# Conditions' blocks on TensorE in four column places, with later loads in the third layer and later states' products in the first

## The chip, the core and the metric

The kernel runs on one core of a Trainium2 chip. The metric is device time in microseconds (us) of one execution; lower is better. Five engines work at once: TensorE (PE, with its weight loads listed as PEld), VectorE (DVE), ScalarE (ACT), GpSimd (POOL) and SyncE (SP). SP, POOL and ACT also issue the transfers (DMA), and a queue issues in order: an issue that waits holds up those behind it.

## The reference, cut to what matters

One step of a diffusion backbone with four layers: a bidirectional state-space scan (SSD), a gated MLP, a second state-space layer (S5) and neighbourhood attention. It works on 128 context tokens and 512 latent tokens of width 1024. Before each layer the two conditions (one for context tokens, one for latent tokens) give shift, scale and gate:

```
mod = silu(cond) @ w_mod[i] + b_mod[i]          # cond: (2, 1024), w_mod[i]: (1024, 3072)
shift, scale, gate = split(mod, 3)
u = (rms_norm(x) * g * (1 + scale) + shift) @ w_in[i]
x = x + gate * (mixer(u) @ w_out[i])
```

So for each of four layers a 2 x 1024 matrix is multiplied by a 1024 x 3072 matrix in float32. The kernel does it in 24 blocks of 512 output columns, six for each layer; a block has 8 tiles of 128 x 512 weights, 2 MB, which are loaded from memory.

## The kernel before, in words

**Large products.** Each projection is a list of units (8 weight tiles of 128x128, 512 KB). `stream` (L326) plays them on TensorE in slots: one slot is six matmuls, two halves of 320 tokens by three terms of a split into high and low parts. `play` takes the order of TensorE from a table written by hand: `put(slot, work)` lets `work` issue its instructions after that slot. TensorE's order is always that of the table. The order of DVE, ACT and POOL is the table's too in the third layer (`ALSO5`); elsewhere, and for SP everywhere, a planner decides it by its own costs. `unit` turns a loaded weight tile (`raw`, 2 buffers) into high and low parts: ACT writes both, and POOL issues a transfer that adds the raw tile to the low part (`wlo<-raw`).

**The conditions' blocks.** `mod_pe` (L388) makes four blocks of the first layer on TensorE before the first projection: the stationary operand is 128x2 (`self.cs`, two conditions), the moving operand a 128x512 weight tile, 8 of them for a block. The other 20 blocks are made beside other work by `mod_ew` (L406), a generator that `tick` advances: two in the first layer's scan, four in its output projection (`leave(0)`), two at the start of the MLP (L1193 to L1198), and six in each of `leave(1)` and `leave(2)`. There DVE does 16 passes for a block over 128x512 elements (L437, L439) into the accumulator `wacc`; TensorE then turns the two sums in 8 transposes of 128x128 (L417), and DVE reduces them (L418). `mod_b` adds the bias. The loads (`wm`, 512 KB each) are asked for one at a time, two ahead.

**The first layer's scan.** Eight groups of heads follow each other on TensorE, 48 slots apart (L944 to L961). In a group, `begin` loads the state H and the decays, `turn` transposes five chunks and DVE makes the weighted copy `xw` (L1047), `context` and `advance` multiply into states (L1077), `off` multiplies states by C (L1112), and `diag` does the part within a chunk (L1068). `tables` at the start makes the step sizes (L804 to L874).

**The third layer.** For 16 items the input side loads matrices (`load_in`, tile `ix`, 3 buffers), transposes them and drives the states (`drive`); DVE steps through the scan (L1768, L1771). The output side loads (`load_out`), generates (`gen`, tiles `gx`), copies states (`take`), multiplies (`answer`), forms a kernel `KK`, spreads it in 8 small transfers on SP's queue (`unroll`, L1842), and multiplies it by the input `ur` (`within`, L1851). `IN5` and `OUT5` hold the slots of these steps, counted from the item's own.

Of the kernel before, what the change touches and what calls it, by code (L numbers as in the profile page):

```python
# [117 lines left out]
class Net:  # L118
# [235 lines left out]
    def cond(self):  # L354
# [7 lines left out]
        nc.vector.tensor_tensor(self.cs, x, t, op=OP.mult)  # L362

# [6 lines left out]
    def mod_w(self, i, nb, k, n, p, bufs, tag="wm"):  # L370

        w = p.tile([128, n, 512] if tag == "wm" else [128, 2, T], F32, tag=tag, bufs=bufs, name=self.n("wm"))[:, 0:n, 0:512]
        self.nc.sync.dma_start(w, self.I["w_mod"][i, nb, k // 2, :, k % 2:k % 2 + n])
        return w
# [12 lines left out]

    def mod_pe(self, i, p, blocks=range(6), bufs=4, n=1):  # L388

        nc = self.nc  # L390
        for nb in blocks:
            q = self.bank("pmod")
            for k0 in range(0, 8, n):
                w = self.mod_w(i, nb, k0, n, p, bufs)
                for j in range(n):
                    k = k0 + j
                    nc.tensor.matmul(q[:2, :], self.cs[:, k, :], w[:, j, :], start=(k == 0), stop=(k == 7))
            r = p.tile([2, 512], F32, tag="modr", bufs=1, name=self.n("modr"))
            nc.scalar.copy(r, q[:2, :])
            q = self.bank("pmodt")  # L400
            for j in range(4):
                nc.tensor.transpose(q[:, 2 * j:2 * j + 2], r[:, 128 * j:128 * j + 128], self.ident[:2, :2])
            self.mod_b(i, nb, q[:, 0:8].rearrange("p (a b) -> p a b", b=2))
            yield

    def mod_ew(self, i, p, blocks=range(6), bufs=2, tags=("wm", "wacc"), pacc=None):  # L406


        nc = self.nc
        e = nc.vector  # L410

        def total(nb, acc):
            q = self.small([128, 4, 2], "modq")
            for c in range(2):
                t = self.bank("pmod")
                for j in range(4):
                    self.nc.tensor.transpose(t[:, 128 * j:128 * j + 128], acc[:, c, 128 * j:128 * j + 128], self.ident)  # L417
                e.tensor_reduce(q[:, :, c], t.rearrange("p (a b) -> p a b", a=4), axis=AX.X, op=OP.add)  # L418
            self.mod_b(i, nb, q)
        todo = [(nb, kb) for nb in blocks for kb in range(4)]  # L420
        load = lambda s: self.mod_w(i, todo[s][0], 2 * todo[s][1], 2, p, bufs, tags[0])
        ws = [load(s) for s in range(bufs - 1)]
        done = None
        for s, (nb, kb) in enumerate(todo):
            w = ws.pop(0)
            if s + bufs - 1 < len(todo):
                ws.append(load(s + bufs - 1))
            if kb == 0:
                acc = (pacc or p).tile([128, 2, 512] if tags[1] == "wacc" else [128, 2, T], F32, tag="s5gx" if pacc else tags[1],
                                       bufs=2 if pacc else 2 if tags[1] == "wacc" else bufs,  # L430
                                       name=self.n("wacc"))[:, :, 0:512]
            for j in range(2):
                k = 2 * kb + j
                for c in range(2):
                    a = self.cs[:, k, c:c + 1]
                    if k == 0:
                        e.tensor_scalar(acc[:, c], w[:, j], a, 0.0, op0=OP.mult, op1=OP.add)  # L437
                    else:
                        e.scalar_tensor_tensor(acc[:, c], w[:, j], a, acc[:, c], op0=OP.mult, op1=OP.add)  # L439
# [1854 lines left out]
```

## Time and profile before

| | |
|---|---|
| median of 3 runs | 3027.43 us (3025.84 to 3032.1) |
| profiled execution: time | 3024.37 us |
| profiled execution: first to last instruction (span) | 3022.4 us |
| granted TensorE clock, mean | 0.956 |
| TensorE busy | 2747.4 us, 91% |
| VectorE busy | 2085.6 us, 69% |
| ScalarE busy | 1478.1 us, 49% |
| GpSimd busy | 1275.1 us, 42% |

The profiled execution lies 3.1 us under the median. A share over the whole span is a mean over very different stages: the scan of the first layer until about 600 us, its output projection until 733, the MLP until 1183, its output projection until 1311, the third layer until 2091, its output projection until 2237, the attention until 2889, and the last output projection. A stage has its own limit, so a number is read in its stage.

### The profile page before, as it was taken

Reading aid. Unit: us, or ns where it says so; the run is one execution under the profiler, and the core shown is the slowest. Engines: PE = TensorE matmul, PEld = TensorE weight load, DVE = VectorE, ACT = ScalarE, POOL = GpSimd, SP = SyncE. Lnnn points to the kernel's source line nnn. Section 1 sums busy time; section 2 is a strip of 40 time slices with the busy share of each in tenths; the row PEclk is TensorE's granted clock in tenths of the full one; section 3 lists DMA queues with packets and bytes.
Section 4 is the critical chain, followed back from the end, with each engine's and each line's share of the span. In section 5 each row is a group of like instructions: output and inputs, shape, how many; then the busy total and the mean of one; then the engine's idle time right before and its main releaser. Section 6 shows DMA issues by size and latency. Waiting matters only on the chain.

```text
span 3022.4 us, 50482 instructions
## 1 busy us (share of the span) xinstructions
PE 2747.4 (91%) x18412; PEld 2636.6 (87%) x18412; DVE 2085.6 (69%) x4948; ACT 1478.1 (49%) x2525; POOL 1275.1 (42%) x1452
## 2 busy tenths in 40 slices
PE   6879989999988888989898876999899999999998
PEld 3768989899988888989898775999889999999998
DVE  5987776676679887735888972225957777777842
ACT  5534434534443444356675553444136666666641
POOL 4466667512576663123443540223343333333332
PEclk9989999999999999999898887999999999999999
DMA  7666667797676667967676569324525444444342
GB/s 254 170 182 164 174 164 192 191 288 220 172 215 194 164 194 227 278 184 219 164 221 169 147 172 186 106 92 135 202 86 148 133 135 131 136 129 135 111 181 85
DMA packets 271734, 517.91 MB, mean 171 GB/s; under 512 B 77888, under 2 KB 146944, under 8 KB 270464
## 3 DMA queue, kind: packets, MB, share of 16 engines
q1 hardware_dynamic: 240512, 411.93, 44.5%
q0 software_dynamic: 24064, 87.04, 14.9%
q10 hardware_dynamic: 6912, 15.73, 1.4%
q8 instruction: 146, 2.39, 0.3%
q14 instruction: 100, 0.82, 0.1%
HBM read 333.83 MB, written 65.70 MB: 132 GB/s over the span
## 4 chain that ended last, share of the span: by engine, by line
PE 31%; DVE 25%; DMA 13%; POOL 9%; ACT 8%; issue 7%; SPq 1%; ACTq 0%; POOLq 0%; DVEq 0%
PE acc L326 25%; DMA wlo<-raw 4%; DVE S L1771 3%; DVE wacc L439 2%; DVE sl L1768 2%; DVE e L2077 2%; DVE cacc L915 2%; POOL dd L1022 2%; POOL dd L1029 2%; ACT e L2075 1%; DMA raw<-in_w_mlp_dram 1%; DVE sb L2072 1%; DMA raw<-in_w_out_dram 1%; DVE pt L205 1%; DVE yn L2108 1%
## 5 line engine op out<-in xcount | busy, mean ns | idle before, releaser
L326 PE MATMUL acc<-hhi,whi 128*128 128x320 f32 (+2 forms) x3472 | 624.2, 319 | 25.4 <-DVE x L610 10.2
L326 PE MATMUL acc<-hlo,whi 128*128 128x320 f32 (+2 forms) x3472 | 633.0, 319 | 2.5 <-DVE hlo L579 1.3
L326 PE MATMUL acc<-hhi,wlo 128*128 128x320 f32 (+2 forms) x3472 | 613.9, 318 | 6.8 <-DMA wlo<-raw 6.8
L326 PEld LDWEIGHTS acc<-hhi,whi 128*128 128x128 f32 (+1 forms) x3472 | 542.7, 193 | 35.3 <-issue 14.6
L326 PEld LDWEIGHTS acc<-hhi,wlo 128*128 128x128 f32 (+1 forms) x3472 | 544.8, 194 | 13.2 <-DMA wlo<-raw 8.7
L326 PEld LDWEIGHTS acc<-hlo,whi 128*128 128x128 f32 (+1 forms) x3472 | 544.7, 193 | 7.9 <-DVE hlo L579 2.8
L226 POOL DMA_DIRECT2D wlo<-raw x164 | 145.1, 891 | 541.8 <-ACT wlo L225 491.9
L205 POOL TENSOR_TENSOR wlo<-raw,whi 128x1024 fp32r<-128x1024 f32 x95 | 244.6, 2576 | 262.9 <-ACT whi L204 86.7
L227 ACT CAST whi<-raw 128x1024 fp32r<-128x1024 f32 (+1 forms) x164 | 170.6, 1041 | 244.8 <-DMA raw<-in_w_mlp_dram 100.3
L225 ACT ACTIVATE wlo<-raw 128x1024 fp32r<-128x1024 f32 (+1 forms) x164 | 173.2, 1057 | 168.7 <-DMA raw<-in_w_mlp_dram 87.9
L439 DVE SCALAR_TENSOR_TENSOR wacc<-wm,conds,wacc 128x512 f32<-128x512 f32 x280 | 224.7, 855 | 30.4 <-DMA wm<-in_w_mod_dram 30.4
L326 PE MATMUL acc<-y,whi 128*128 128x320 f32 (+2 forms) x1024 | 175.8, 312 | 7.1 <-DVE y L746 3.1
L1771 DVE TENSOR_TENSOR S<-S,sl 128x32 f32<-128x32 f32 x1008 | 176.4, 230 | 0.0
L204 ACT CAST whi<-raw 128x1024 fp32r<-128x1024 f32 x125 | 129.2, 1046 | 76.0 <-PE acc L326 67.8
L326 PEld LDWEIGHTS acc<-y,whi 128*128 128x128 f32 x1024 | 155.5, 188 | 10.6 <-DVE y L746 4.5
L2077 DVE TENSOR_SCALAR e<-e,mx 128x384 f32<-128x384 f32 (+1 forms) x160 | 154.1, 963 | 4.2
L915 DVE SCALAR_TENSOR_TENSOR cacc<-pad,vec,cacc 128x644 f32<-128x644 f32 x128 | 144.2, 1127 | 2.2 <-ACT cacc L913 0.9
L2075 ACT ACTIVATE e<-sb,mx 128x384 f32<-128x384 f32 x128 | 79.0, 617 | 107.3 <-DVE mx L2074 106.6
L1768 DVE TENSOR_TENSOR sl<-S,A 128x64 f32<-128x64 f32 x504 | 120.9, 280 | 0.0
L1889 DVE TENSOR_TENSOR y<-y,sg 128x640 f32<-128x640 f32 x16 | 14.1, 879 | 150.2 <-ACT sg L1888 150.2
L1547 POOL TENSOR_TENSOR s5gy<-Bu,Qt 128x512 f32<-128x512 f32 x64 | 90.0, 1438 | 57.3 <-DVE s5gx L1557 53.9
L1022 POOL TENSOR_TENSOR dd<-cmat,dt 128x512 f32<-128x512 f32 x80 | 108.2, 1358 | 12.2 <-DVE dt L826 9.4
(407 smaller groups left out, 5381.9 us busy)
## 6 DMA issues: line engine op xcount, KB each, us to landing
wlo<-raw POOLq DMA_DIRECT2D x163, 512.0 KB, 5.4
wm<-in_w_mod_dram SPq DMA_DIRECT2D x96, 512.0 KB, 6.5
raw<-in_w_out_dram SPq DMA_DIRECT2D x64, 512.0 KB, 4.5
raw<-in_w_nat_dram SPq DMA_DIRECT2D x64, 512.0 KB, 3.8
raw<-in_w_ssd_dram SPq DMA_DIRECT2D x48, 512.0 KB, 3.5
raw<-in_w_mlp_dram SPq DMA_DIRECT2D x48, 512.0 KB, 3.6
fb<-fd SPq DMA_DIRECT2D x40, 512.0 KB, 5.4
s5X<-s5gx SPq DMA_DIRECT2D x32, 512.0 KB, 4.8
```

The costliest lines, as they stand in the source:

```text
L204: (hi_eng or nc.scalar.copy)(hi, src)
L205: (lo_eng or nc.vector).tensor_tensor(lo, src, f(hi), op=OP.subtract)
L225: self.nc.scalar.activation(lo, raw, AF.Copy, scale=-1.0)
L226: self.nc.gpsimd.dma_start(lo, raw, accum_op=OP.add)
L227: self.nc.scalar.copy(hi, raw)
L326: mm(p[:m, o:o + c], w[:, kt, :], v(hx), start=(k == 0 and wi == 0), stop=(k == 8 * len(units) - 1 and wi == 2))
L439: e.scalar_tensor_tensor(acc[:, c], w[:, j], a, acc[:, c], op0=OP.mult, op1=OP.add)
L915: nc.vector.scalar_tensor_tensor(acc, pad[:, j:j + 644], w(j), acc, op0=OP.mult, op1=OP.add)
L1022: nc.gpsimd.tensor_tensor(dg.rearrange("p (h l) -> p h l", h=4), N.ident[:, None, :].to_broadcast([128, 4, 128]), self.dt[:, c, 32 * d + 4 ...
L1768: e.tensor_tensor(t[d], F[:, d, at[d], None, :].to_broadcast([128, 2, 32]), A[:, :, d], op=OP.mult)
L1771: e.tensor_tensor(dst[d], dst[d], t[d][:, k].rearrange("p (r g) -> p r g", r=2)[:, ::1 - 2 * k], op=OP.add)
L2077: nc.vector.tensor_scalar(e[:, :w], e[:, :w], m[:, 3:4], None, op0=OP.mult)
```

## The change

Every condition block goes to TensorE. `self.csx` is the conditions with zeros behind; a stationary operand is now 32 columns of it, of which two are the conditions of this tile, and the others give sums that nobody reads. Tile k writes to the output partitions 32*(k%4) to 32*(k%4)+31. `mod_end` sums the four places and transposes in one: four products of 128 columns of the copy `r` with `sel`, a 128x2 matrix that is one where the partition modulo 32 is 0 or 1. In `mod_ew` the four loads of a block are asked for together, right after the products of the block before; products are issued at every fourth tick, and `mod_end` one tick after the ACT copy. The tick times stay.

```diff
+    def mod_sums(self, ws):
+        q = self.bank("pmod")
+        for k, w in enumerate(ws):
+            o = 32 * (k % 4)
+            self.nc.tensor.matmul(q[o:o + 32, :], self.csx[:, 2 * k:2 * k + 32], w, start=(k < 4), stop=(k >= 4))
+        return q
+    def mod_end(self, i, nb, r):
+        q = self.bank("pmodt")
+        for j in range(4):
+            self.nc.tensor.matmul(q[:, 2 * j:2 * j + 2], r[:, 128 * j:128 * j + 128], self.sel, start=True, stop=True)
+        self.mod_b(i, nb, q[:, 0:8].rearrange("p (a b) -> p a b", b=2))
...
     def mod_pe(self, i, p, blocks=range(6), bufs=4, n=1):
         for nb in blocks:
+            ws = [self.mod_w(i, nb, k, n, p, bufs) for k in range(0, 8, n)]
+            q = self.mod_sums([w[:, j, :] for w in ws for j in range(n)])
+            r = p.tile([128, 512], F32, tag="modr", bufs=1, name=self.n("modr"))
+            self.nc.scalar.copy(r, q)
+            self.mod_end(i, nb, r)
...
+    def mod_ew(self, i, p, blocks=range(6), tags=("wm", "modr"), more=None):
+        lend = lambda: more[0].tile([128, 2, 512], F32, tag=more[1], bufs=2, name=self.n("wm"))
+        load = lambda nb: [self.mod_w(i, nb, 2 * kb, 2, p, MB if more else 4, tags[0], lend if more and kb == 3 else None)
+                           for kb in range(4)]
+        blocks = list(blocks)
+        ws, done = load(blocks[0]), None
+        for n, nb in enumerate(blocks):
             yield
+            if done:
+                self.mod_end(i, *done)
+                done = None
+            yield
+            yield
+            q = self.mod_sums([w[:, j, :] for w in ws for j in range(2)])
...
+            self.nc.scalar.copy(r, q)
+            done = nb, r
+            if n + 1 < len(blocks):
+                ws = load(blocks[n + 1])
+            yield
+        self.mod_end(i, *done)
         yield
...
-            put(t - 2, self.begin, N, P)
+            put(t + 2, self.begin, N, P)
...
-            put(t + 5, self.context, N, P)
-            for j, s in enumerate((1, 2 * TA + TS, 4 * TA + TS, 4 * TA + 2 * TS + 1)):
+            put(t + 10, self.context, N, P)
+            for j, s in enumerate((1, 2 * TA + TS + 2, 4 * TA + TS + 2, 4 * TA + 2 * TS + 3)):
                 if j:
                     put(t + s - 3, self.fade, N, P, j)
                     put(t + s, self.advance, N, P, j)
-                put(t + s + TS + (4 if j else 0), self.off, N, P, j)
+                put(t + s + TS + 4, self.off, N, P, j)
...
-IN5 = (-3, -1, 1, 4, 9, 12)
-OUT5 = (-15, 0, -5, 0, 5, 7, 9, 17)
+IN5 = (-2, -1, 1, 5, 9, 12)
+OUT5 = (-10, 0, -5, 0, 5, 7, 9, 19)
...
-                put(e + IN5[s], self.load_in, P, s)
+                for d in range(2):
+                    put(e + (2 if s == d == 1 else IN5[s]), self.load_in, P, s, d)
...
                 put_(o + OUT5[0], self.load_out, P)
+                put_(o + 6, self.load_again, P)
...
-                put_(o + OUT5[6] + 3, self.unroll, P)
+                put_(o + OUT5[6] + 2, self.unroll, P)
                 put_(o + OUT5[7], self.within, P)
...
     def load_out(self, N, P):
-        P["ur"] = self.load_u(N, kt)
...
+    def load_again(self, N, P):
+        P["ur"] = self.load_u(N, P["kt"])
```

In the MLP and in `leave(1)` the fourth tile of a block and the copy `r` borrow buffers of other tags (`s5gx`, `wacc`), since `wm` has three there. In `leave(2)` tiles and copies lie in the buffers `ya` and `yb`.

## Rows read from the trace of the kernel before

**Rows 1.** The page: two engines, the costliest condition group, and the condition loads
```profile
PE 2747.4 (91%) x18412; PEld 2636.6 (87%) x18412; DVE 2085.6 (69%) x4948; ACT 1478.1 (49%) x2525; POOL 1275.1 (42%) x1452
...
L439 DVE SCALAR_TENSOR_TENSOR wacc<-wm,conds,wacc 128x512 f32<-128x512 f32 x280 | 224.7, 855 | 30.4 <-DMA wm<-in_w_mod_dram 30.4
...
wm<-in_w_mod_dram SPq DMA_DIRECT2D x96, 512.0 KB, 6.5
```

**Rows 2.** Busy time by stretch: length, busy us (instructions) by engine, then clock, DMA
```profile
core 0: us, PE busy (x) PEld busy (x) DVE busy (x) ACT busy (x) POOL busy (x), PEclk, DMA share, GB/s
62.00:200.00 138.00, 110.31 (x709) 104.16 (x707) 124.27 (x148) 67.80 (x106) 68.89 (x50) 0.90 0.66 175
200.00:585.00 385.00, 353.03 (x2433) 332.33 (x2431) 270.74 (x299) 166.46 (x265) 255.02 (x215) 0.96 0.69 174
626.00:716.00 90.00, 89.30 (x619) 88.78 (x618) 62.34 (x103) 29.99 (x34) 10.41 (x12) 1.00 0.94 275
1202.00:1291.00 89.00, 89.00 (x618) 88.78 (x616) 69.40 (x118) 28.22 (x30) 10.52 (x12) 1.00 0.93 274
2091.00:2207.00 116.00, 106.57 (x711) 106.03 (x710) 113.10 (x139) 24.28 (x29) 49.81 (x15) 0.96 0.55 185
2904.00:2991.00 87.00, 86.74 (x591) 86.47 (x590) 19.40 (x24) 20.38 (x24) 28.91 (x12) 1.00 0.37 128
1320.00:1820.00 500.00, 432.76 (x3041) 424.30 (x3040) 373.41 (x1690) 303.64 (x504) 209.53 (x331) 0.91 0.67 182
```

**Rows 3.** TensorE's groups by form: count, busy us, mean ns, idle before
```profile
L1112 PE MATMUL off<-c,H 128*128 128x128 f32 x256 | 34.4, 279 | 10.4 <-DVE H L1101 10.1 <-DVE y L1071 0.2
L1068 PE MATMUL yd<-dd,xb 128*64 128x128 f32 x320 | 26.3, 285 | 0.7 <-ACT off L1084 0.7
L417 PE MATMUL pmod<-cmat,wacc 128*128 128x128 f32 x160 | 22.1, 281 | 1.0 <-DVE wacc L439 1.0
```

**Rows 4.** TensorE in order of time, setup stage: start, us, instructions
```profile
30.27 1.28 PE L469 MATMUL cols<-ones,ssum 128*128 128x1 f32 x10
...
33.44 7.03 PE L397 MATMUL pmod<-wm,conds 128*2 128x512 f32 x16
```

**Rows 5.** GpSimd in order of time, setup stage (columns as in Rows 4)
```profile
46.86 1.86 POOL L226 DMA_DIRECT2D wlo<-raw x2
```

**Rows 6.** What TensorE waited for from 62 to 200 us: total, times, longest
```profile
PE G L1054 <- DVE xw L1047: 7.9, 2, 7.3
PE stc L1077 <- DVE xw L1047: 7.1, 1, 7.1
PE dtT L823 <- DVE dtv L816: 3.3, 1, 3.3
PE G L1054 <- DVE y L1071: 3.0, 1, 3.0
```

**Rows 7.** The same from 200 to 585 us
```profile
PE st L1077 <- DVE xw L1047: 4.3, 4, 1.3
PE stc L1077 <- DVE xw L1047: 3.7, 2, 2.1
```

**Rows 8.** TensorE in order of time in the third layer's output projection
```profile
2125.59 3.54 PE L326 MATMUL acc<-hhi,whi 128*128 128x320 f32 x12 [6.56 <-DVE x L610]
...
2190.65 3.77 PE L326 MATMUL acc<-hhi,whi 128*128 128x320 f32 x16 [2.87 <-DVE x L610]
```

**Rows 9.** What TensorE waited for most from 1320 to 1820 us
```profile
PE t L1851 <- DMA tr<-KK: 33.5, 9, 7.2
```

**Rows 10.** What SP's queue waited for in the same stretch
```profile
SPq L1794 <- DVE gx L1544: 63.6, 10, 14.8
SPq L1695 <- PE mT L1708: 54.8, 22, 5.2
SPq L1842 <- ACT KK L1836: 37.5, 9, 6.0
```

**Rows 11.** Busy time from the first scan to the last (columns as in Rows 2)
```profile
1390.00:1800.00 410.00, 350.34 (x2456) 343.50 (x2455) 358.51 (x1663) 247.93 (x402) 195.62 (x310) 0.90 0.65 179
```

More of the change, by code (lines that the diff above doesn't have):

```diff
@@ L362, in cond @@
         nc.vector.tensor_tensor(self.cs, x, t, op=OP.mult)
+        self.csx = c.tile([128, 48], F32, name="condsx")
+        nc.vector.memset(self.csx, 0.0)
+        nc.vector.tensor_copy(self.csx[:, 0:16], self.cs.rearrange("p k c -> p (k c)"))
+        self.sel = c.tile([128, 2], F32, name="sel")
+        nc.sync.dma_start(self.sel, self.I["consts"][:, 664:666])
     def mod_tiles(self, i):
@@ L388, in mod_pe @@
     def mod_pe(self, i, p, blocks=range(6), bufs=4, n=1):
-        nc = self.nc
         for nb in blocks:
[L392 to L403, printed above, removed]
-            yield
@@ L406, in mod_ew @@
[L406 to L439, printed above, removed]
-            yield
-            if kb == 1 and done:
-                total(*done)
-            if kb == 3:
-                done = nb, acc
-                if pacc:
-                    total(*done)
-                    done = None
-        if done:
-            total(*done)
@@ new lines, in mod_pe @@
+            ws = [self.mod_w(i, nb, k, n, p, bufs) for k in range(0, 8, n)]
[3 more added lines that the diff above has]
+            self.mod_end(i, nb, r)
+            yield
+    def mod_ew(self, i, p, blocks=range(6), tags=("wm", "modr"), more=None):
[5 more added lines that the diff above has]
+        for n, nb in enumerate(blocks):
+            yield
+            if done:
[4 more added lines that the diff above has]
+            q = self.mod_sums([w[:, j, :] for w in ws for j in range(2)])
+            if more:
+                r = lend()[:, 0]
+            elif tags[1] == "modr":
+                r = p.tile([128, 512], F32, tag="modr", bufs=1, name=self.n("modr"))
+            else:
+                r = p.tile([128, 2, T], F32, tag=tags[1], bufs=4, name=self.n("modr"))[:, 0, 0:512]
+            self.nc.scalar.copy(r, q)
[4 more added lines that the diff above has]
+        self.mod_end(i, *done)
@@ L661, in leave @@
             self.rest = i == 0
-            self.put_beside(self.mod_ew(i + 1, self.tp, blocks, bufs=4 if mod else MB, tags=mod or ("wm", "wacc")))
+            self.put_beside(self.mod_ew(i + 1, self.tp, blocks, tags=mod or ("wm", "modr"), more=(self.tp, "wacc") if i == 1 else None))
             for s in range(4 * len(blocks) + 4):
@@ L1195, in groups @@
             mod = []
-            put(RM[0] - 1, lambda: mod.append(N.mod_ew(1, self.tp, (4, 5), MB, pacc=N.tp)))
+            put(RM[0] - 1, lambda: mod.append(N.mod_ew(1, self.tp, (4, 5), more=(N.tp, "s5gx"))))
             for k in range(10):
@@ L1690, in load_u, with load_in @@
         return ur
-    def load_in(self, N, P, s):
-        for d in range(2):
-            x = P["in", s, d] = self.tile(N, [128, 4, 128], "ix", BI)
-            N.nc.sync.dma_start(x, N.s5X[2 * P["kt"] + s][:, d])
+    def load_in(self, N, P, s, d):
+        x = P["in", s, d] = self.tile(N, [128, 4, 128], "ix", BI)
+        N.nc.sync.dma_start(x, N.s5X[2 * P["kt"] + s][:, d])
     def gen(self, N, P, s):
@@ L2131 @@
     NVEC += _w
-NCONST = 664
+NCONST = 666
 def net(ctx, tc, I, O, layers=(0, 1, 2, 3)):
@@ L2196, in layout @@
                                   i[:, None] <= i, i[:, None] >= i, i[:, None] > i, i[:, None] < i,
-                                  i[:, None] // 8 == i[:16]], 1).astype(np.float32)
+                                  i[:, None] // 8 == i[:16], i[:, None] % 32 == i[:2]], 1).astype(np.float32)
     r["w_mod"] = np.ascontiguousarray(a["w_mod"].reshape(4, 4, 2, 128, 6, 512).transpose(0, 4, 1, 3, 2, 5))
```

10 lines of the change are left out of this document (6 added, 4 removed).

## The prediction, made before the changed kernel ran

> **What bounds the kernel now.** First the busy shares [rows 1]: TensorE is busy 2747 of 3022 us, so at most 275 us are idle, and DVE is busy 2086 us, of which the passes over the condition blocks are 225 us. A share of the span doesn't tell what they are worth, so next comes the busy time by stretch [rows 2]. Read two columns against each other, TensorE and DVE. In the first scan's opening (62 to 200 us) DVE has 124 of 138 us, TensorE 110: DVE sets the pace. In the scan's later part TensorE has 353 of 385. In the middle of the output projections of layers one and two (the 90 and 89 us stretches) TensorE has no idle time at all, and transfers fill 0.94 and 0.93 of the 16 engines. In the third layer's output projection DVE has 113 of 116 us, TensorE 107. The last projection, which has no condition blocks, gives the undisturbed rate: 591 matmuls in 86.74 us, 0.147 us each, or 0.88 us for a slot of six. The third layer has 67 us without TensorE work in 500, and a granted clock of 0.91. So DVE relief is worth something in two of the five places where blocks are made, and nothing in the 90 and 89 us stretches, where new TensorE work is paid in full. Last come TensorE's own waits, which say what ended each idle time; they are named with their stretch below.
>
> **What a block costs TensorE.** Removed: 8 transposes for a block, 22.1/160 = 0.138 us each [rows 3], 1.1 us. Added: 8 products over 512 columns. The same products with two stationary columns stand in the setup: 16 passes (each float32 product is two) in 7.03 us, 0.44 us for a pass [rows 4]. How many run abreast in four column places no row shows for four. The nearest rows are for two places: `yd` (64 columns, two places) takes 26.3/320 = 0.082 us for a pass over 128 columns, `off` (all 128 columns, one place) 34.4/256 = 0.134 [rows 3]. Eight passes of `yd` take 0.66 us; four at `off`'s price are 0.54, so two places run wholly abreast, with 0.12 us for changing over. Bounds for a block: 7.03 us if the places take turns, 3.5 if only two run abreast, 4 x 0.44 + 0.12 = 1.9 if all four do. I take 1.9, since the two-place row shows full overlap. The new sum of the places (`mod_end`) is four float32 products with a 128x128 stationary and two moving columns; the nearest row has ten passes with one moving column in 1.28 us [rows 4], so eight cost 1.0 us. A block is 2.9 us instead of 1.1: **1.8 us more**, 36 us for 20 blocks.
>
> The two-place row shows twofold overlap. The Trainium skill, page "TensorE: Matmul & The Clock Gate", section on packing small matmuls, has less: three column tiles with 512 columns give 2.38 times. At that share (0.79 of the count) a block's products would take, by estimate, 7.03/3.17 = 2.2 us plus the change, 0.46 us more, and the sum below would end 9 us higher.
>
> **Setup.** Four blocks lose 5 us each of TensorE time. I count it at nothing: the low parts of the first weights are issued by GpSimd, at 46.9 us, when its own table work is done [rows 5], and the change doesn't touch that. If ACT's copies get an earlier place, up to 10 us are won (estimate).
>
> **First layer's scan (two blocks).** DVE loses 28 us of its 124 in the opening. The waits for it there are 7.9 + 7.1 + 3.3 + 3.0 = 21.3 us [rows 6]: xw copies that came late, and step sizes that stood behind condition passes. `context` five slots later gives 4.4 us to the 7.1 us wait, `advance` two slots later 1.8 us to each `st`. In the later part st and stc wait 8.0 us [rows 7]. Of moved steps: `begin`'s three loads on SP go 4 slots later, but so does the first `off` that reads them; context's ACT copy and store, and the first `off`'s DVE product and two GpSimd adds move 4 or 5 slots, with nothing but the group's own end behind. I take two thirds of 29.3, since what follows an ended wait is often late itself: -19.5. The clock of 0.90 over 138 us means a fifth of the time at 1.2 GHz, 13.8 us lost; waits gone give some back: -3.5. Two blocks: +3.6. **-19.4**; bounds +3.6 and -40.
>
> **First output projection and MLP (four and two blocks), second (six).** No idle time to win [rows 2]. 12 x 1.8 = **+21.6**. Then the loads. A late load used to stop DVE, 30.4 us in all [rows 1], which TensorE didn't feel; now TensorE's order is fixed, `mod_sums` waits for eight tiles, and all weight products queue behind it. A block's period is four ticks of 4.6 slots, 16.2 us. In it the transfers carry 2.1 MB of conditions, and for 2.3 units 2.4 MB (raw and low part): 4.5 MB at 274 GB/s, 16.4 us. It just fits, as the stretches show by 0.93. The loads are issued a full period ahead, and land in 6.5 us undisturbed [rows 1]. I take **+6**; bounds 0 and +30.
>
> **Third output projection (six blocks).** DVE's queue held the residual update back, and TensorE stood 6.6 and 2.9 us, then ran 12 and 16 matmuls in 3.54 and 3.77 us instead of 1.8 and 2.4, at 1.2 GHz [rows 8]: together 12.5 us, which the relief removes. Against it 6 x 1.8 = 10.8. **-1.7**. Transfers have room there, 0.55.
>
> **Third layer's loads.** `within` waits 33.5 us in nine places for the transfer tr [rows 9]. It is asked for one slot earlier and used two later; the 256 slots of this input projection fill the stretch, 2 us each, so the chain KK, eight issues, landing gets 6 us more against a longest wait of 7.2. SP's queue stands 63.6 us on load_out (L1794, until gen frees its buffer), 54.8 on ix (L1695) and 37.5 on KK [rows 10], and holds up what is behind. Moved five slots later, load_out meets a free buffer; the fourth ix load, and `ur`, which now holds its buffer for 13 slots instead of 32, likewise. unroll's eight issues move ahead by one slot, so weight loads behind them can wait longer for KK. Two thirds of 33.5: -22.3; clock, at half the share of idle time removed (45 us lost at 0.91, a third of the idle gone): -7.5. **-29.8**. The bound on the gain: DVE is busy 358.5 of 410 us there [rows 11], so not over 51; against: 0, or +5 if loads asked for later come late.
>
> **Sum.** -19.4 + 21.6 + 6 - 1.7 - 29.8 = -23.3 us on 3024.4 gives 3001; the median of the runs stands 3.1 us higher: **3004 us**.
>
> **Rivals.** *The places don't all run abreast.* With two abreast a block costs 1.6 us more, 20 blocks 32: 3036; with none 5.1 more: 3106. The forecast's gain is eaten at 23.3/20 = 1.2 us, that is when the products of a block take over 3.1 us. For it: no row has four. Against: `yd`. *TensorE takes over DVE's wait for loads.* All 30 us instead of 6: 3028, within the bound of no change. For it: 0.93 and 0.94. Against: a full period of lead. *The gaps fill again:* in scan and third layer other waits take the place of the removed ones, because DVE (0.90 and 0.87 busy) sets the pace anyway. Then only costs are left, 3.6 + 21.6 + 6 - 1.7, 29 us more: 3057. It decides where DVE's idle time in the third layer stays under 10 of 410 us. *More than forecast:* all named waits go, -40 and -45: 2973.
>
> **Chances.** Forecast 0.50 (2985 to 3022); more than forecast 0.14; loads waited for 0.13; two abreast 0.11; gaps fill again 0.07; none abreast 0.05. The range of 8 in 10 takes in the deep case, the loads and two abreast: 2968 to 3044. A measurement tells some 0.2% (6 us) from no change. Faster (under 3021): 0.14 + 0.48 = 0.62; within it (3021 to 3033): 0.15; slower: 0.23.
>
> **What would show it.** The new passes start in fours, and a block's 16 passes take about 2 us at full clock: right; 3.5 or 7: the first rival. TensorE's waits for wm under 10 us in all. The 90 and 89 us stretches longer by 7 to 12 us for the same weight products. TensorE's wait for tr from 33.5 to near 10, SP's on L1794 from 63.6 to under 20. The gap before stc of 7.1 us gone. Wrong would be: the scan as long as before with DVE 28 us emptier, or `y` and `drv` waiting instead of `t`.

## The result, and the profile of the changed kernel

The changed kernel takes 3061.4 us (median; 3056.0 to 3064.1), the kernel before 3028.5 in the same comparison: a ratio of 1.0101, 95% interval 1.0087 to 1.0115. The change makes the kernel 31 us slower. The forecast was 3004, with a range to 3044: the sign was wrong, and the time lies outside the range. The profiled execution took 3059.7 us.

First the page: the busy time of the engines, and the queue that carries most of the transfers (packets, MB, share of 16 engines' span).

```profile
PE 2771.8 (91%) x18748; PEld 2645.8 (87%) x18748; DVE 1821.7 (60%) x4590; ACT 1487.0 (49%) x2543; POOL 1249.6 (41%) x1452
...
q1 hardware_dynamic: 240656, 411.93, 45.7%
```

Against [rows 1], VectorE has lost 264 us of work and TensorE has gained 24. So 264 us were taken off one engine, 24 put on the other, and the kernel became 31 us longer: whatever VectorE's relief was worth, more was paid for it.

The stages are cut at the first weight product of each, in both traces (the same products can be counted in both). All in us:

| stage | before | after | difference | forecast |
|---|---|---|---|---|
| until the first weight product | 48.5 | 44.5 | -4.0 | 0 |
| first layer's scan | 551.5 | 549.8 | -1.7 | -19.4 |
| its output projection (4 blocks) | 133.3 | 144.0 | +10.7 | +7.2 |
| MLP (2 blocks) | 449.9 | 466.8 | +16.9 | +3.6 |
| its output projection (6 blocks) | 127.9 | 138.9 | +11.0 | +10.8 |
| third layer, scan part | 508.1 | 509.6 | +1.5 | -29.8 |
| third layer, gated unit | 271.5 | 273.1 | +1.6 | 0 |
| its output projection (6 blocks) | 146.6 | 145.6 | -1.0 | -1.7 |
| attention and last projection | 770.0 | 770.7 | +0.7 | 0 |

The forecast's +6 for loads belonged to the MLP and the two projections beside it together. The table ends at the last weight product, 15 us before the end in both. One stage of one execution scatters: over the runs below, stages with the same instructions in the same order differ by 5 us and sometimes 9 (the MLP took 447.0 us in e2 and 455.8 in e16). A single row of this table under that says little; the medians of the runs decide.

The same stages by windows (columns as in [rows 2]), from the first scan to the third layer:

```profile
core 0: us, PE busy (x) PEld busy (x) DVE busy (x) ACT busy (x) POOL busy (x), PEclk, DMA share, GB/s
44.50:594.30 549.80, 488.57 (x3301) 459.76 (x3297) 372.08 (x427) 243.76 (x388) 326.19 (x274) 0.94 0.72 181
594.30:738.30 144.00, 140.40 (x952) 130.39 (x952) 48.00 (x84) 55.16 (x74) 17.81 (x22) 0.97 0.78 227
738.30:1205.10 466.80, 412.74 (x2716) 401.23 (x2715) 326.41 (x694) 203.51 (x259) 279.53 (x448) 0.95 0.69 187
1205.10:1344.00 138.90, 135.17 (x932) 124.13 (x931) 30.79 (x56) 50.26 (x64) 17.75 (x21) 0.99 0.80 229
1344.00:1853.60 509.60, 428.85 (x3074) 418.65 (x3072) 373.21 (x1701) 309.94 (x516) 211.99 (x338) 0.92 0.69 182
```

The kernel before, first scan and third layer's scan part:

```profile
48.50:600.00 551.50, 483.52 (x3270) 453.81 (x3269) 405.85 (x464) 246.42 (x388) 328.12 (x269) 0.94 0.69 178
1311.10:1819.20 508.10, 438.08 (x3074) 428.83 (x3072) 377.80 (x1703) 310.36 (x517) 213.79 (x338) 0.91 0.67 183
```

In the two short stages VectorE is now busy for a third and less, and they are the ones that got longest for their size: TensorE has 140.4 of 144.0 and 135.2 of 138.9 us. (The first ran at a granted clock of 0.97, before at 1.00; in e1 below, at 1.00, it took 140.5 us, the forecast's +7.2.) In the scan and the third layer TensorE still has 61 and 81 idle us (before, 68 and 70). That is where the forecast's gain was to come from.

**The blocks themselves** came out as forecast. TensorE in order of time, second output projection (start, us, line, instructions):

```profile
1242.58 1.63 PE L326 MATMUL acc<-yhi,wlo 128*128 128x320 f32 x10
1244.13 1.93 PE L400 MATMUL pmod<-wm,condsx 128*32 128x512 f32 x16
...
1254.01 0.95 PE L407 MATMUL pmodt<-sel,wm 128*128 128x2 f32 x8
```

Sixteen passes over 512 columns take 1.93 us, changing over included, against 7.03 one after the other [rows 4]: four places run wholly abreast (forecast 1.9). Nineteen of the 24 blocks take 1.92 or 1.93 us; the setup's four and the first of the scan take 2.2 to 5.5, three of these at a granted clock of 0.50 to 0.58. `mod_end` takes 0.95 (forecast 1.0). The Trainium skill (page "TensorE: Matmul & The Clock Gate", section on packing small matmuls) has 2.38 times for three column places, by which the forecast's text estimated 2.2 us plus the change; the trace has 3.6 times for four, so here the measurement is better than that figure.

### The profile page after: what moved, and what is told of

It is laid out like the page before. It is cut to its first block, busy times and chain, and to the rows that moved or that the text cites. A ratio compares the mean times of both kernels' runs of the same rounds, so it can differ in the third digit from the quotient of the medians.

```text
span 3057.9 us, 50796 instructions
## 1 busy us (share of the span) xinstructions
PE 2771.8 (91%) x18748; PEld 2645.8 (87%) x18748; DVE 1821.7 (60%) x4590; ACT 1487.0 (49%) x2543; POOL 1249.6 (41%) x1452
## 3 DMA queue, kind: packets, MB, share of 16 engines
q1 hardware_dynamic: 240656, 411.93, 45.7%
## 4 chain that ended last, share of the span: by engine, by line
PE 43%; DVE 23%; DMA 9%; ACT 6%; issue 6%; POOL 5%; SPq 1%; ACTq 0%; DVEq 0%; POOLq 0%
PE acc L326 35%; DVE S L1769 4%; DVE sl L1766 3%; DMA wlo<-raw 2%; DVE e L2078 2%; DVE cacc L912 2%; DMA raw<-in_w_mlp_dram 1%; ACT e L2076 1%; DVE sb L2073 1%; DVE yn L2109 1%; DVE pt L205 1%; PE pmod L400 1%; PE S L2067 1%; DMA fb<-fd 1%; PE drv L1733 1%
## 5 line engine op out<-in xcount | busy, mean ns | idle before, releaser
L326 PE MATMUL acc<-hhi,whi 128*128 128x320 f32 (+2 forms) x3472 | 618.8, 319 | 37.5 <-ACT hhi L204 20.5
L326 PE MATMUL acc<-hlo,whi 128*128 128x320 f32 (+2 forms) x3472 | 633.9, 319 | 2.6 <-DVE hlo L576 1.7
L326 PE MATMUL acc<-hhi,wlo 128*128 128x320 f32 (+2 forms) x3472 | 620.7, 319 | 14.0 <-DMA wlo<-raw 14.0
L326 PEld LDWEIGHTS acc<-hhi,whi 128*128 128x128 f32 (+1 forms) x3472 | 539.2, 192 | 48.9 <-ACT hhi L204 21.5
L326 PEld LDWEIGHTS acc<-hhi,wlo 128*128 128x128 f32 (+1 forms) x3472 | 546.7, 194 | 20.3 <-DMA wlo<-raw 15.4
L326 PEld LDWEIGHTS acc<-hlo,whi 128*128 128x128 f32 (+1 forms) x3472 | 543.0, 192 | 13.2 <-issue 5.1
L205 POOL TENSOR_TENSOR wlo<-raw,whi 128x1024 fp32r<-128x1024 f32 x95 | 230.1, 2422 | 272.4 <-PE acc L326 95.2
L326 PE MATMUL acc<-y,whi 128*128 128x320 f32 (+2 forms) x1024 | 177.8, 313 | 6.3 <-DVE y L205 2.8
L326 PEld LDWEIGHTS acc<-y,whi 128*128 128x128 f32 x1024 | 156.6, 189 | 12.1 <-DVE y L205 4.0
L607 DVE SCALAR_TENSOR_TENSOR x<-acc,mod,x 128x128 f32<-128x128 f32 (+3 forms) x53 | 29.3, 595 | 226.7 <-PE acc L326 225.2
L912 DVE SCALAR_TENSOR_TENSOR cacc<-pad,vec,cacc 128x644 f32<-128x644 f32 x128 | 146.7, 1146 | 9.5 <-ACT cacc L910 8.2
L2109 DVE TENSOR_TENSOR yn<-yn,av 64x128 f32<-64x128 f32 x320 | 90.6, 283 | 32.4 <-ACT yn L2107 23.6
```

What stands on the lines that cost most here:

```text
L205: (lo_eng or nc.vector).tensor_tensor(lo, src, f(hi), op=OP.subtract)
L326: mm(p[:m, o:o + c], w[:, kt, :], v(hx), start=(k == 0 and wi == 0), stop=(k == 8 * len(units) - 1 and wi == 2))
L912: nc.vector.scalar_tensor_tensor(acc, pad[:, j:j + 644], w(j), acc, op0=OP.mult, op1=OP.add)
L2109: nc.vector.tensor_tensor(y[r, o], y[r, o], p[r, w:w + 128], op=OP.add)
```

## The experiments

Theory A at the outset: in the scan and the third layer something other than the removed waits sets the pace, so only costs are left (the forecast's rival with a chance of 0.07). Theory B: the blocks are worth what was forecast, and one of the groups of moved slots spoils it. Ratios are to the kernel before, measured beside each run. The medians are shown in us; 0.1% is 3 us.

### e1 to e4: each part alone

e1 has the blocks' hunks of the diff alone, e2 the scan's slots alone (`begin`, `context`, `advance`, `off`), e3 the third layer's hunks alone. e4 makes the four blocks of the setup and the two in the scan on TensorE and leaves the other 18 on VectorE, by the generator of before under another name (`mod_old`):

```diff
+    def mod_old(self, i, p, blocks=range(6), bufs=2, tags=("wm", "wacc"), pacc=None):
...
+            self.put_beside(self.mod_old(i + 1, self.tp, blocks, bufs=4 if mod else MB, tags=mod or ("wm", "wacc")))
...
+            put(RM[0] - 1, lambda: mod.append(N.mod_old(1, self.tp, (4, 5), MB, pacc=N.tp)))
```

> The conditions' blocks on TensorE alone: the slots of the first layer's scan and the loads of the third layer stay as before. Theory A (DVE and the table of slots set the pace of the scan and of the third layer, so the blocks bring only their cost): the time is that of the changed kernel, 3061 us within 6, with the output projection of layer one, the MLP and its output projection together 35 to 40 us longer than before, and the third layer within 3 us of before. Theory B (the blocks are worth what was forecast, and one of the two groups of moved slots spoils it): 3000 to 3045 us, that is faster than the changed kernel by over 15 us.

> Only the moved slots of the first layer's scan (begin, context, advance, off), with the blocks still on DVE. Forecast's view: the two waits for xw in the opening lose some 6 us, so 3021 to 3025 us. Theory A: DVE sets the pace of the scan, and what is taken off the one wait is lost at the next or at the group's end: 3025 to 3035 us, with the last group's products reaching further into the output projection.

> Only the moved loads, unroll and within of the third layer, with the blocks still on DVE. Forecast's view: that stage 20 to 30 us shorter, 2998 to 3008 us. Theory A: TensorE's waits for tr go (33.5 to under 6 us), and others of the same size come (r, KT, zr), the stage stays at 508 to 511 us: 3027 to 3032 us.

> Blocks on TensorE only for the first layer itself (four in the setup, two in the scan's opening); the other 18 stay on DVE; no slots are moved. Theory A, with the stages of the changed kernel's trace: setup 4 us shorter, scan 0 to 20 us shorter, everything behind as before: 3004 to 3025 us. Forecast's view: the scan keeps what its opening wins: 3004 to 3010 us. If what the opening wins is given back in the scan whatever the slots are: 3022 to 3026 us.

| | median, us | ratio, 95% interval |
|---|---|---|
| e1 blocks alone | 3051.3 | 1.0065 (1.0046 to 1.0084) |
| e2 scan's slots alone | 3031.6 | 1.0006 (0.9993 to 1.0018) |
| e3 third layer's moves alone | 3029.3 | 1.0003 (0.9990 to 1.0017) |
| e4 blocks of setup and first scan alone | 3031.0 | 1.0003 (0.9986 to 1.0020) |

No part alone makes the kernel faster, and e1 with e2 and e3 is 22 us, not 31: the parts don't simply add. The times of e2 and e3 came out as theory A said; e4 lies above all three of its ranges. e1 missed both expectations: it lies 10 us under the changed kernel, so a group of moved slots costs something beside the blocks.

**The third layer (e3)** shows why its 30 us did not come. TensorE's largest waits in that stage:

```profile
PE mT L1709 <- DVE r L1856: 20.3, 2, 10.7
PE y L1827 <- ACT zr L1614: 17.2, 7, 7.7
PE KT L1836 <- ACT kk L1828: 13.4, 3, 7.1
PE mT L1709 <- DMA ix<-s5X: 5.7, 3, 3.0
PE t L1855 <- DMA tr<-KK: 4.3, 4, 1.6
```

The wait for tr went from 33.5 us [rows 9] to 4.3, as the forecast's step said, and others took its place. Before, from 1311 to 1820 us, two of them were smaller, and there was none behind kk:

```profile
PE y L1823 <- ACT zr L1614: 12.1, 7, 6.7
PE mT L1708 <- DVE r L1852: 4.4, 1, 4.4
```

The longest, 10.7 us, can be followed on the two engines. TensorE first, then VectorE:

```profile
1492.38 1.91 PE L1855 MATMUL t<-ur,tr 128*128 128x80 f32 x16
1494.08 1.13 PE L326 MATMUL acc<-hlo,whi 128*128 128x320 f32 x6
1495.05 0.60 PE L1709 MATMUL mT<-cmat,ix 128*128 128x128 f32 x4
1506.35 1.11 PE L1709 MATMUL mT<-cmat,ix 128*128 128x128 f32 x4 [10.70 <-DVE r L1856]
```

```profile
1494.38 0.36 DVE L1769 TENSOR_TENSOR sl<-S,A 128x64 f32<-128x64 f32 x2
1494.65 0.53 DVE L1772 TENSOR_TENSOR S<-S,sl 128x32 f32<-128x32 f32 x4
...
1498.00 1.28 DVE L1544 TENSOR_TENSOR gx<-BC,PQ 128x512 f32<-128x512 f32 x2
1499.20 1.79 DVE L1557 TENSOR_TENSOR gx<-gx,gy 128x512 f32<-128x512 f32 x2
...
1505.80 0.89 DVE L1856 TENSOR_TENSOR r<-yk,t 128x320 f32<-128x320 f32 x2
```

`within`'s products t are done at 1494.3. VectorE's `r`, which empties their two banks, runs at 1505.8: in the table's order it now stands behind a run of scan steps and four passes of `gx`, 11 us of work that needs nothing from t. All small products share four banks in rotation (`bank`, L184), so the next transposition mT waits for `r`. VectorE is busy without a break in these 11 us, but only 373 of the stage's 512 us; the order on it is what costs here.

The wait for kk, 13.4 us and new, is the same cause at one remove. Further on in e3, on ACT and then on TensorE:

```profile
1724.99 0.74 ACT L1858 ACTIVATE r<-r 128x640 f32<-128x640 f32 x1 [15.76 <-DVE r L1856]
...
1728.08 0.26 ACT L1828 COPY kk<-y 128x128 f32<-128x128 f32 x1
```

```profile
1728.89 0.69 PE L1836 MATMUL KT<-cmat,kk 128*128 128x128 f32 x2 [7.13 <-ACT kk L1828]
```

ACT's own `r` (L1858), which reads VectorE's late `r`, stands at the head of ACT's queue for 15.8 us, and kk behind it. So nearly all of 33.7 us of the stage's waits (20.3 and 13.4) hang on the late `r`; the wait for zr (17.2) was not traced.

**The scan (changed kernel, e2)** has the same kind of thing. The gap of 7.1 us before stc is gone [rows 6], and in the changed kernel there stands instead, from 44 to 594 us:

```profile
PE xbT L1040 <- ACT x L913: 27.4, 7, 5.4
```

Before, from 44 to 600 us, it was:

```profile
PE xbT L1043 <- ACT x L916: 2.4, 3, 1.1
```

In the changed kernel it comes seven times in eight groups, and in e2, without the blocks, it is 28.0 us in seven. One of them on VectorE, ACT and TensorE:

```profile
299.09 1.22 DVE L1022 TENSOR_TENSOR_SCAN dd<-fb,dd 128x512 f32<-128x512 f32 x1 [2.53 <-POOL dd L1019]
300.23 3.45 DVE L912 SCALAR_TENSOR_TENSOR cacc<-pad,vec,cacc 128x644 f32<-128x644 f32 x3
303.60 0.68 DVE L1098 TENSOR_TENSOR H<-H,st 128x512 f32<-128x512 f32 x1
304.20 0.88 DVE L912 SCALAR_TENSOR_TENSOR cacc<-pad,vec,cacc 128x644 f32<-128x644 f32 x1
```

```profile
305.11 0.31 ACT L913 ACTIVATE x<-cacc 128x128 f32<-128x128 f32 x1 [7.46 <-DVE cacc L912]
```

```profile
301.13 0.27 PE L1040 MATMUL xbT<-cmat,x 128*128 128x128 f32 x1
305.48 0.48 PE L1040 MATMUL xbT<-cmat,x 128*128 128x128 f32 x1 [4.08 <-ACT x L913]
```

`advance`'s sum H (L1098), two slots later than before, stands ahead of the last of four passes of the next group's convolution (L912); ACT's x follows the last pass, and `turn`'s transposition follows x. Whether that is the cause, e17 tests.

### e5 and e9: the third layer's moves, taken apart

Both leave the blocks on VectorE. e5 is e3 with `within` in its old slot; e9 also has the input loads in their old slots.

```diff
-OUT5 = (-10, 0, -5, 0, 5, 7, 9, 19)
+OUT5 = (-10, 0, -5, 0, 5, 7, 9, 17)
```

```diff
-IN5 = (-2, -1, 1, 5, 9, 12)
+IN5 = (-3, -1, 1, 4, 9, 12)
...
-                    put(e + (2 if s == d == 1 else IN5[s]), self.load_in, P, s, d)
+                    put(e + IN5[s], self.load_in, P, s, d)
```

> The third layer's moved loads and the earlier unroll as in e3, but within stays in its old slot (17 instead of 19); blocks on DVE. Theory B (the two slots of within are what spoils that stage: TensorE's products t end, but DVE's r that empties their bank now stands behind a batch of scan steps, and the next transposition mT waits for that bank, 10.7 and 9.6 us in e3): those two waits go, the waits for tr lie between 5 and 25 us, and the time is 3012 to 3022 us. Theory A (DVE sets the pace of that stage whatever the slots are): new waits of the same sum elsewhere, 3026 to 3033 us.

> As e5 (third layer alone, within in its old slot), and the input side's loads ix back in their old slots too; left of the change are load_out five slots later, ur's own later load, and unroll one slot earlier. In e5 TensorE's waits for ix rose from 2.7 to 12.6 us. Theory B (each moved step is paid where its own reader then waits): the ix waits return to under 5 us, the time falls to 3012 to 3020 us. Theory A (the sum of waits in that stage is kept by DVE): 3021 to 3028 us, as e5, with the waits under other names.

e5: 3024.0 us, ratio 0.9981 (0.9967 to 0.9996). e9: 3029.9 us, 0.9999 (0.9982 to 1.0017). TensorE's waits, e5 and then e9:

```profile
PE t L1855 <- DMA tr<-KK: 18.8, 7, 6.1
PE mT L1709 <- DMA ix<-s5X: 12.6, 6, 3.2
PE t L1855 <- DVE sl L1769: 11.2, 2, 5.7
```

```profile
PE t L1855 <- DMA tr<-KK: 26.4, 8, 5.5
PE mT L1709 <- DVE r L1856: 9.6, 2, 5.6
PE t L1855 <- DVE S L1772: 6.7, 1, 6.7
```

With `within` back, the two stalls behind `r` of 20.3 us are 5.2 us, as theory B said, and those behind kk are gone in e5 and e9, but ix rises to 12.6 and `within` itself now waits 11.2 us for VectorE. With the loads back, ix is small again and tr is 26.4. The stage took 512.2 us in e3, 509.8 in e5, 511.1 in e9 and 508.1 before. Theory A's wording "DVE sets the pace" goes too far (VectorE is busy 350 of the 410 us that answer to [rows 11] in the changed kernel); but its number holds: in four orders of these steps TensorE's idle time in that stage is 70 to 81 us, under other names. e5's 3024.0 us lie between the ranges of both theories, e9's 3029.9 above both. e5's 6 us are the only gain seen, and e9, nearer to the old order, did not have them; which step brings them stays open.

### e8: the MLP's two blocks

e1 with the MLP's two blocks back on VectorE (`mod_old` in the line of `RM`).

> e1 with the MLP's two blocks back on DVE; the other 18 later blocks and the setup on TensorE, no moved slots. Theory C (the two blocks of the MLP cost 14 us there, not 3.6: their 2 MB of loads at once, and TensorE's wait for them, hold up the transfers of the low parts): the MLP returns to 447 to 453 us and the time to 3035 to 3041 us. Theory K (the MLP is longer for another reason, such as the clock it inherits): it stays at 460 to 466 us, 3047 to 3053 us.

3045.4 us, 1.0055 (1.0036 to 1.0074), and the MLP is 454.6 us instead of 464.2. The stage goes part of the way to theory C; the ratio falls by 0.10%, 3 us, which the intervals can't tell from the forecast's 3.6 nor from nothing. TensorE's wait for low parts (L326 for wlo) in the MLP falls from 10.3 us in e1 to 5.8. So the two blocks cost some 3 to 10 us there, and not the whole of the 14. (Time and MLP both lie between the ranges of the two theories, and e8's tiles lie 224 bytes displaced, e1's 160, which the sections below show to matter.)

### e6, e7, e10, e11: a gain that didn't last

e4's trace had the setup 3.4 and the scan 11.0 us shorter, yet the time was that of before: the MLP, the third layer and the gated unit, with the same instructions in the same order on every engine, came out 5, 8 and 5 us longer. e6 has only the new constants, which nobody reads:

```diff
+        self.csx = c.tile([128, 48], F32, name="condsx")
...
+        self.sel = c.tile([128, 2], F32, name="sel")
+        nc.sync.dma_start(self.sel, self.I["consts"][:, 664:666])
...
-NCONST = 664
+NCONST = 666
```

e7 is e4 once more. e10 is e4 with `sel` summed on VectorE, so that the array of constants in memory stays as it was:

```diff
-        nc.sync.dma_start(self.sel, self.I["consts"][:, 664:666])
+        nc.vector.tensor_reduce(self.sel, self.ident.rearrange("p (a b) -> p b a", a=4)[:, 0:2, :], axis=AX.X, op=OP.add)
```

e11 is e10 with e9's moves.

> The kernel before with only the new constants (condsx, sel and two more columns of the constants in memory), which nobody reads; everything else as before. Theory P (where tiles and arrays lie costs something): e4's stages behind the scan, whose order of instructions is that of before, were 20 us longer than before in the trace, so a part of that shows here: 3036 to 3048 us. Theory N (those 20 us are the scatter of single executions, mostly of the granted clock): 3027 to 3033 us.

> The kernel of e4 once more. If the 20 us behind the scan are scatter, its stages come out otherwise this time: output projection, MLP, third layer within 4 us of before, and the profiled execution at 3012 to 3020 us. If what the scan wins (11 us) is given back later in every execution, the median is 3026 to 3034 us again, and the stages with a lower granted clock (MLP 0.95, third layer 0.90, GLU 0.91) show it again.

> The kernel of e4 and e7, but the 128x2 matrix sel is summed on DVE from the identity that is there anyway; the array of constants in memory keeps its 664 columns, and one transfer less is issued. Theory M (the 5 us of e6 come from where arrays lie in memory): 3016 to 3023 us. Theory S (from where tiles lie in the core's memory, which is as in e6, or from chance): 3024 to 3031 us.

> e9 and e10 together: blocks on TensorE in the setup and the first scan, sel summed on DVE, and of the third layer's moves only load_out, ur and unroll. If the two gains add: e10's time less what e9 gains, 3006 to 3018 us. If what one stage gains is given back in the next: 3020 to 3028 us.

| | median, us | ratio, 95% interval |
|---|---|---|
| e6 | 3035.1 | 1.0022 (1.0005 to 1.0039) |
| e7 | 3026.8 | 0.9997 (0.9986 to 1.0008) |
| e10 | 3036.6 | 1.0027 (1.0012 to 1.0041) |
| e11 | 3036.3 | 1.0028 (1.0012 to 1.0043) |

Two tiles that nobody reads cost 7 us (2 to 12), with one load and two short instructions in the setup, which was 1.6 us longer in e6's trace; the time lies 1 us under theory P's range and 2 above theory N's. The array in memory is not the cause (e10). e10 and e11 miss all their ranges, on the slow side. And e10 is 0.24 and 0.30% slower than e4 and e7 (beyond the intervals against e7), though every engine's order is theirs but for `sel` and one DVE product in the first 7 us, and its tiles lie where theirs do. Nothing here explains that, so a difference of 0.3% between two kernels is not yet a cause. The gated unit of the third layer was 273.0 to 276.1 us in the nine kernels so far that have the new tiles, and 268.1 to 271.5 in before, e2, e3, e5 and e9, which don't. What the tiles do is move every later tile of the core's memory: `raw` begins at byte 23552 = 92 x 256 of each partition before, and it and nearly all tiles behind it are displaced alike. `condsx` takes 192 bytes and `sel` 32, so 224 in e4, e6, e7, e8, e10 and e11; the changed kernel, e1 and e12 no longer hold `conds` (64 bytes), so 160.

### e13 to e16: the displacement

e13, e14 and e15 are the changed kernel, e1 and e4 with `sel`'s tile made longer, so that the displacement is 256 bytes (32 columns in e13 and e14, 16 in e15). e16 is the kernel before with 32 idle bytes.

```diff
-        self.sel = c.tile([128, 2], F32, name="sel")
+        self.sel = c.tile([128, 32], F32, name="sel")[:, 0:2]
```

```diff
+        nc.vector.memset(c.tile([128, 8], F32, name="idle"), 0.0)
```

> The changed kernel, with the tile of sel made 128 bytes long, so that all later tiles lie 256 bytes behind their place in the kernel before instead of 160. Theory D (transfers into tiles that don't begin at a multiple of 256 bytes take longer; that is part of what the change lost): 3046 to 3056 us, the GLU at 268 to 272 us and the loads of gyl at 4.4 us from issue to landing. Theory N (the displacement does nothing): 3058 to 3064 us, GLU 273 to 276.

> e1 (all blocks on TensorE, no moved slots) with the displacement of 256 bytes instead of 160. Theory D: 3036 to 3046 us, MLP 448 to 458 us instead of 464. Theory N: 3047 to 3054 us.

> e4 and e7 (blocks on TensorE in the setup and the first scan alone) with the displacement of 256 bytes instead of 224. Theory D: what the scan and the setup win stays, 3012 to 3022 us, with the third layer at 507 to 511 us and the GLU at 268 to 272. Theory N: 3026 to 3034 us.

> The kernel before with one idle tile of 32 bytes, so that all later tiles lie 32 bytes further; one memset more. Theory D: 3032 to 3040 us, as e6, GLU 273 to 276 us. Theory N: 3026 to 3032 us, GLU 268 to 272.

| | displaced otherwise | by 256 bytes |
|---|---|---|
| changed kernel | 1.0101 (1.0087 to 1.0115) | e13: 3053.5 us, 1.0082 (1.0068 to 1.0096) |
| blocks alone | e1: 1.0065 (1.0046 to 1.0084) | e14: 3039.8 us, 1.0035 (1.0022 to 1.0049) |
| first layer alone | e4, e7: 1.0003, 0.9997 | e15: 3020.8 us, 0.9973 (0.9959 to 0.9987) |

e16: 3032.9 us, 1.0010 (1.0000 to 1.0020). All three kernels gain 0.2 to 0.3%, 6 to 9 us. The intervals of each pair overlap a little or touch, and the two kernels of a pair ran in different sessions, each against the kernel before there (e1 and e14, e4, e7 and e15 on different chips); that three pairs go the same way carries it, and e10 shows that one pair would not. e16 alone is at the edge of nothing. The stages follow only in part: the gated unit is 270.9 and 269.4 us in e13 and e14 and 275.0 in e16, as expected by D, but 273.6 in e15, where 268 to 272 was expected, and 272.5 and 272.9 in e17 and e18 below; and the third layer's scan part is 515.6 us in e13, against 509.6 in the changed kernel. The transfers show it directly. The hardware queues' row of e13, of e16 and of the kernel before:

```profile
q1 hardware_dynamic: 240656, 411.93, 44.2%
```

```profile
q1 hardware_dynamic: 240512, 411.93, 45.0%
```

```profile
q1 hardware_dynamic: 240512, 411.93, 44.5%
```

Share times span: the same 412 MB took 1345 us of 16 engines' time before, 1397 in the changed kernel (45.7% of 3057.9), 1350 in e13 and 1363 in e16. The changed kernel's packets took 3.9% longer, and 256 bytes of displacement give it back. All kernels here divide by it: 1344 to 1358 us in the ten with a displacement of 0 or 256 bytes, 1363 to 1397 in the ten with another. The loads of `gyl` (issues, KB, us to landing), before and e16:

```profile
gyl<-y5d SPq DMA_DIRECT2D x32, 80.0 KB, 4.4
```

```profile
gyl<-y5d SPq DMA_DIRECT2D x32, 80.0 KB, 5.1
```

The Trainium skill (page "DMA: Bandwidth & Descriptors", section on how a descriptor splits into AXI transactions) says of a read that its pieces have at most 256 bytes and must start at multiples of 256, so that one which begins between them can need one piece more (4 instead of 3 in its example of 576 bytes). The direction agrees with these rows. That this is the mechanism is argued here: no run counts the pieces, and most of these transfers write into the displaced tiles (333.8 MB are read from memory in all, 65.7 written to it), of which that section says nothing. Nor is it shown through which waits the longer transfers reach the time.

### e12 and e17: the scan's slots beside the blocks

e12 is e1 with all of the scan's moved slots. e17 is e14 with `begin`, `context` and the first `off` moved, but `advance`, its `fade` and the offs behind it in their old slots:

```diff
-            for j, s in enumerate((1, 2 * TA + TS + 2, 4 * TA + TS + 2, 4 * TA + 2 * TS + 3)):
+            for j, s in enumerate((1, 2 * TA + TS, 4 * TA + TS, 4 * TA + 2 * TS + 1)):
```

> The changed kernel without the third layer's moves: all blocks on TensorE, and the first scan's moved slots. Theory B (the scan's slots cost, since the group's last products then push the next group's convolution back on DVE): 3056 to 3063 us, against 3051 of e1. If the 10 us between e1 and the changed kernel come from the third layer's moves: 3048 to 3054 us.

> e14 (all blocks on TensorE, displacement of 256 bytes) with the scan's moved begin, context and first off, but advance and the offs behind it in their old slots. Theory H (advance's two slots cost): TensorE's waits for ACT's x under 8 us instead of 28, the waits of stc from xw gone, and 3034 to 3042 us, as e14 (3040) or better. If context and off are at fault: the waits for x stay above 20 us, 3046 to 3054 us.

e12: 3059.6 us, 1.0111 (1.0094 to 1.0128), against 1.0065 of e1: beside the blocks the scan's slots cost 14 us. It lies where the changed kernel lies, so the third layer's moves bring and cost nothing there either. e17: 3033.6 us, 1.0020 (1.0007 to 1.0033), against 1.0035 of e14. TensorE's waits in e17's scan:

```profile
PE off L1109 <- DVE H L1098: 8.0, 4, 3.2
PE xbT L1040 <- ACT x L913: 5.9, 5, 1.8
```

The waits for x fall from 28 to 5.9 us (4.8 in e14), and the scan takes 528.5 us: 541.4 in e14, 550.7 in e13 with `advance` moved, 551.5 before. So `context`, `begin` and the first `off` later, with the blocks gone from VectorE, win what the forecast wanted of the scan and more (23 us in the trace), and `advance`'s two slots, with the `fade` and the offs that go with it, take it away. Not all of it reaches the end: e17's time can't be told from e14's, since the intervals overlap, and its MLP was 463.7 us, 6.6 longer than e14's. Why the MLP is long when the scan ends early is open.

### e18: the best of it

e15 with e5's moves of the third layer: blocks on TensorE only in the setup and the first scan, tiles displaced by 256 bytes, all of the third layer's moves but `within`'s.

> e15 (blocks on TensorE in the setup and the first scan, displacement of 256 bytes) with e5's moves in the third layer (all but within). If what e5 won (6 us) adds: 3012 to 3018 us. If DVE sets the pace of the third layer whatever its loads do: 3018 to 3025 us.

3017.0 us, 0.9960 (0.9945 to 0.9975): 12 us faster than the kernel before, and by the ratios 43 faster than the changed one. Against e15 the intervals overlap. e17's slots were not tried on top of it.

## Why the prediction was wrong

By its own terms, with the ratios turned into us at 3029:

- **Products in four places, 1.9 us, and `mod_end`, 1.0: right** (1.93 and 0.95). The rival of places that take turns was wrong.
- **Late blocks, +21.6 and +6 for loads, -1.7 in the third projection, 25.9 in all: about right.** e14 less e15, the same 18 blocks, is 0.62%, 19 us. In the changed kernel TensorE waited nowhere for `wm` after the setup; "TensorE takes over DVE's wait for loads" was wrong. In the two short projections, e14 and e15 by windows:

```profile
585.40:725.90 140.50, 136.45 (x945) 127.02 (x944) 47.27 (x83) 54.76 (x73) 17.84 (x22) 1.00 0.81 239
...
1183.00:1318.20 135.20, 133.33 (x932) 122.54 (x932) 30.70 (x56) 49.99 (x64) 17.82 (x21) 1.00 0.81 237
```

```profile
586.40:721.90 135.50, 129.78 (x881) 126.44 (x879) 91.16 (x153) 52.05 (x68) 17.20 (x22) 0.99 0.86 248
...
1175.80:1301.90 126.10, 122.49 (x836) 121.45 (x836) 96.53 (x161) 46.08 (x58) 17.63 (x21) 0.99 0.86 254
```

Four blocks put 6.7 us on TensorE, six put 10.8: 1.7 and 1.8 us a block, the forecast's 1.8. VectorE empties by 44 and 66 us beside it, and the stages get 5 and 9 us longer. For the MLP, "No idle time to win" had no row behind it: TensorE was busy 404 of its 450 us before.

- **Setup at nothing: 4 us better**, 3 to 6 in each kernel with the blocks.
- **First scan, -19.4: the relief was there, the slots were mis-stepped.** e15, without moved slots, is 8 us faster than before (4 to 12), and the trace's scan 10 us shorter. The failing step is "`advance` two slots later 1.8 us to each `st`", counted as gain alone: the list "Of moved steps" asks what stands behind `begin`, `context` and the first `off`, and leaves `advance` out. Its sum H is VectorE's, whose queue holds two groups at once, and behind a later H stands the next group's convolution. The price was 27 us of waits for x, 14 us in the time (e12 against e1). The steps that were listed did no harm where they were moved without `advance` (e17). The forecast's sign of being wrong came: the scan as long as before (549.8 us against 551.5) with VectorE 34 us emptier.
- **Third layer, -29.8: wrong, 0 measured** (e3 1.0003; e12 against the changed kernel). The chain to tr was sized rightly, 33.5 to 4.6 us. The failing step is "used two later": the forecast asked who issues into the moved slot and which queues it passes on SP, but not behind what the moved product's consumer on VectorE then stands, how many banks its output holds meanwhile, nor what waits behind that consumer on ACT. That came to 33.7 us of waits for `r` and kk in e3, which all but vanish in e5. But `within` in its old slot waits for tr and VectorE instead, so "two thirds of 33.5" failed with it: the measured share was none, and the clock's -7.5 went the same way, since TensorE's idle time did not fall (70 us before, 81 after). SP's wait on load_out fell from 63.6 to 31.9 us, not under 20, and `y` waits 18.0 us for zr, 12.1 before: the forecast's other sign of being wrong.
- **The displacement: absent from the forecast**, 6 to 9 us. The two tiles were read as free. That it costs is shown in the transfers; its size in the time rests on three pairs.

Together: first scan and setup -8, its slots +14, late blocks +19, third layer 0 to -3, displacement +6 to +9, some 30 us; measured 31. (In the forecast's own sums, "more than forecast" comes to 2968, not 2973; nothing hangs on it.) The forecast's rival "the gaps fill again" gave 3057, with a chance of 0.07; its number was near, but its condition (VectorE's idle time under 10 of 410 us) was not: it was 60. The gaps that could be traced filled because of the order on VectorE, with idle time left.

## What to carry to other kernels

When a step is moved in a hand-written order, list for each of its outputs the engine that consumes it, what stands ahead of that consumer in the new order and what behind it, and how many buffers are held until then; a wait that is removed is worth only what the next consumer in line leaves. Taking work off an engine that isn't the limit of its stage gives nothing, and the work costs its full price where the other engine has no idle time: here the same exchange won 8 us in the setup and the first scan and lost 19, taken together, in the four later stages, and should have been made in the first two alone. Before an edit is blamed for a stage that it doesn't touch, see whether its new tiles have moved everybody else's.

## What the runs showed of the hardware

Four column places of 32 columns ran fully abreast in float32: 16 passes over 512 columns in 1.93 us, 0.12 us per pass. And the place of the tiles within the core's memory shows in the transfers: displaced by 160 bytes from where the kernel before has them, the same 412 MB took 2.7 to 3.9% more transfer time (e1, e12, the changed kernel), by 224 bytes 1.4 to 2.3%, by 32 bytes 1.3%, and by 256 at most 1.0%. The page's queue rows show it and no engine's row does. Three pairs put it at 0.2 to 0.3% of the kernel's time.
